# Token mixers that give way to the dense products half as often, in a two-layer hybrid encoder

## The chip, the core and the metric

The kernel runs on one core of one Trainium2 chip. The metric is the device time of one execution in microseconds (us), as the median of several runs. The kernel works on five engines: TensorE (PE in the profile; PEld is its weight load), VectorE (DVE), ScalarE (ACT), GpSimd (POOL) and SyncE (SP, which only issues DMAs here).

## The reference, cut to what matters

Input and output are 512 tokens of 1024 float32 numbers. Two layers follow one another, and a last RMSNorm. Each layer runs four token mixers A, B, C and D side by side on one projection, merges them by gates, and adds an MLP:

```python
for l in range(DEPTH):                       # DEPTH = 2
    xn = rmsnorm(x, norm1_g[l])
    h = xn @ w_in[l]                         # 1024 -> all mixers' inputs, split by columns
    y_a = gdn_mixer(...)                     # gated DeltaNet, both directions, 4 heads of 128
    y_b = diff_mixer(b_q, b_k, b_v, ...)     # softmax minus lam * softmax, 4 heads, full attention
    y_c = swa_mixer(c_q, c_k, c_v, ...)      # +-128 window, 8 query heads on 2 kv heads, sinks
    y_d = mlstm_mixer(...)                   # matrix memory, both directions, 4 heads
    branch = einsum('bsnw,nwd->bsnd', stack([y_a, y_b, y_c, y_d]), w_branch[l])
    gate = sigmoid(einsum('bsd,dne->bsne', xn, w_gate[l]))
    x = x + sum(gate * branch, axis=2) @ w_out[l]
    xn = rmsnorm(x, norm2_g[l])
    x = x + square(relu(xn @ w_mlp1[l])) @ w_mlp2[l]      # 1024 -> 4096 -> 1024
```

For the parts of the kernel that the change touches: the mLSTM (D) weighs `exp(decay) * (q k)` for each pair of tokens, multiplies it with v, and divides by a norm; B takes two softmax maps per head, p0 - lam p1, times v; C is a softmax over a band of up to three blocks of 128 keys, times v. B and D end with an RMSNorm over each head.

## The kernel before, in words

**Two streams on one TensorE.** The first stream is the dense one: the input projection, gates, branch projections, output projection and MLP, cut into *items*. Each product is taken in three passes over a high and a low part of both factors (lines 441, 442, 443 for moving tiles of 512 columns, lines 398, 399, 400 for 256 columns). Weights come from memory by DMA into one of two buffers `wr` (line 281), ACT rounds them to `wh` (line 298), DVE takes the rest `wl` (line 299). An item yields after each small group of its matmuls: mostly 6 of 512 columns or 12 of 256. The second stream is the mixers, generators that issue a few small matmuls (128 to 512 columns) with the ACT, DVE and POOL work around them, and then yield a number of nanoseconds.

**What sets the order.** `drive` (line 347) steps a mixer; the number that it yields goes to `fill` (line 332), which adds it to a debt and issues dense groups until the debt is paid. A larger number makes the next dense stretch longer. The numbers stand in the table `G` (`dh=1000`, `ds=1500`, `b1=900`, `b2=1100`, `b3=700`, `c=950`, `ce=1100`, `ss=300`). After that a scheduler orders the instructions on each engine by their order of issue and by when their operands are expected, so ACT, DVE and POOL rows can also move when only the yields change. Finished head norms of B go into a list `pend` and are transposed (`y_T`, line 1146, its matmuls line 1149) a few dense groups later. PSUM is shared by two pools of four banks: `pd` for the dense stream and `pm` for the mixers.

**The mixers, in the order in which they run in each layer (lines 1692 to 1702).** A (line 1157) has a loop `ss` that squares 8 tiles and adds them up by matmuls, and yields after each (line 1202). D (line 1446): for each head, four *s* groups (lines 1486, 1487: the score tile; 1493: the exps `W` on ACT; 1496: the product with the scores on DVE), each followed by a yield (line 1498), and four *hout* groups of the head before (line 1460: 10 small matmuls in all for one block of 128 tokens; 1462 to 1467: division by the norm, into `hs`), each followed by a yield (line 1468). After the last hout, the head norm (lines 1134 to 1145: squares on POOL 1138, sums on DVE 1140, a root on DVE 233 and POOL 234, products on DVE 1142 and 1143) and four `y_T`. B (line 1515) runs twice, for two heads each (B0 and B1 below), over 8 units: `front` (1529, 1530 scores; 1531 maximum on DVE; 1533 exps on ACT), three units later `mid` (1544 transposes, 1546 copy `at` on ACT), five units later `back` (1555 product with v, 1557 `bo` on ACT), with a yield after each. C (line 1583) does the same with 32 units: `front` (1591, 1592; exps 1599; POOL 1603 scales `cp`), three units later `mid` (1615) and `back`.

**Projections beside them.** Rotary inputs of B and C are evacuated by ACT (line 1013, four copies per bank), DVE (1014, 1015), POOL (1016) and put away by ACT and DVE (1024 to 1033).

Of the kernel before, what the change touches and what calls it, by code (L numbers as in the profile page):

```python
# [115 lines left out]
def encoder(ctx: ExitStack, tc: tile.TileContext, a: dict, out: bass.AP, dbg: dict = None):  # L116
# [1040 lines left out]
    def mixer_a(l, L):  # L1157
# [39 lines left out]
        for i, (src, w0) in enumerate(((kb, 72), (qb, 8))):  # L1197
            for h in range(4):
                sq = A(s="sq")
                act.activation(sq, src[:, h, :], AF.Square)  # L1200
                mm(ss, C["ssel"][:, w0 - h:w0 - h + P], sq, start=(i == 0 and h == 0), stop=(i == 1 and h == 3))
                yield G['ss']
        lnr = A(s="lnr")
        act.activation(lnr, ss, AF.Ln, scale=colc(2), bias=colc(7))
        gA = L.gA
# [240 lines left out]
    def mixer_d(l, L):  # L1446
        vx, EM, mb = L.vx, L.EM, L.mb
        qs, kh, kl = [[t[:, h, :] for h in range(4)] for t in (L.dq, L.dkh, L.dkl)]
        hsum = [A(s="hs") for _ in range(NT)]
        Ws = {}  # L1450

        def hout(h):
            W = Ws.pop(h)
            for t in range(NT):
                hb = PSM()
                hv = hb.rearrange("p (d c) -> p d c", d=2)
                for d in range(2):
                    js = range(0, t + 1) if d == 0 else range(t, NT)
                    for j in js:
                        mm(hv[:, d, 0:130], W[d][j][:, blk(t)], vx[:, j, h, :], start=(j == js[0]), stop=(j == js[-1]))  # L1460
                dn = SM(2, "dn")
                act.activation(dn, hv[:, :, 128], AF.Abs)
                dve.tensor_tensor(dn, dn, EM[:, t, h::4], op=ALU.max)
                dve.reciprocal(dn, dn)
                ho = hsum[t][:, blk(h)]
                act.activation(ho, hv[:, 0, 0:128], AF.Copy, scale=dn[:, 0:1])
                dve.scalar_tensor_tensor(ho, hv[:, 1, 0:128], dn[:, 1:2], ho, op0=ALU.mult, op1=ALU.add)
                yield G['dh']

        for h in range(4):  # L1470
            R, Rm = [], []
            for d in range(2):
                r = PSM()
                mm(r, oneh(0, d * 4 + h), L.RB1, start=True, stop=True)
                r1, r2 = A(s="R"), A(s="Rm")
                act.copy(r1, r)
                dve.tensor_tensor(m4(r2), m4(r), bmid(f(neg[1][:, d, :]), 4), op=ALU.add)
                R.append(r1)
                Rm.append(r2)
            yield G['dr']  # L1480
            W = [[None] * 4, [None] * 4]
            if h > 0:
                yield from hout(h - 1)
            for j in range(NT):
                s_ = PSM()
                mm(s_, kh[h][:, blk(j)], qs[h], start=True, stop=False)
                mm(s_, kl[h][:, blk(j)], qs[h], start=False, stop=True)
                for d in range(2):
                    ts_ = range(j, NT) if d == 0 else range(0, j + 1)
                    n = len(ts_)  # L1490
                    w_ = A(s="W") if n > 0 else None
                    for t in ts_:
                        act.activation(w_[:, blk(t)], (Rm if t == j else R)[d][:, blk(t)], AF.Exp,
                                       bias=mb[:, d, j, t, h:h + 1])
                    sl = slice(ts_[0] * P, (ts_[-1] + 1) * P)
                    dve.tensor_tensor(w_[:, sl], s_[:, sl], w_[:, sl], op=ALU.mult)
                    W[d][j] = w_
                yield G['ds']
            Ws[h] = W
        yield G['hl']  # L1500
        yield from hout(3)
        yT = ynew()
        L.y["d"] = yT
        ys = {}
        for tt in range(NT):
            ys[tt] = head_norm(hsum[tt], 4, L.og[:, tt, :].rearrange("p (h c) -> p h c", h=4))
            dump_y(f"yd{l}", ys[tt], 4, tt, 0)
            yield G['yn']
        yield G['yw']
        for tt in range(NT):  # L1510
            y_T(ys.pop(tt), 4, tt, 0, yT)
            yield G['yt']
        marks.add(f"yd{l}")

    def mixer_b(l, L, hp):
# [51 lines left out]
        for i in range(len(units) + b2):  # L1567
            if i < len(units):
                fr[i] = front(*units[i])
                yield G['b1']  # L1570
            if 0 <= i - b1 < len(units):
                md[i - b1] = mid(fr.pop(i - b1))
                yield G['b2']
            if 0 <= i - b2 < len(units):
                y = back(*units[i - b2], md.pop(i - b2))
                if y is not None:
                    pend.append([G['yp'], lambda y=y, u=units[i - b2]: y_T(y, 2, u[0], 2 * hp, yT)])
                yield G['b3']
        if hp == 1:
            L.y["b"] = yT  # L1580
            pend.append([0, lambda: marks.add(f"yb{l}")])
# [1 line left out]
    def mixer_c(l, L):  # L1583
# [60 lines left out]
        for i in range(len(units) + cl + 2):  # L1644
            if i < len(units):
                while f"cqT{units[i][0]}{l}" not in marks:
                    yield 1300
                fr[i] = front(*units[i])
                yield G['c']
            else:  # L1650
                yield G['ce']
            if 0 <= i - cl < len(units):
                mid(*units[i - cl], fr.pop(i - cl))
                yield G['c']
            j = i - cl - 1
            if 0 <= j < len(units) and units[j][2] == 3:
                u = units[j]
                back(u[0], u[1], u[3])
                yield G['c']
        L.y["c"] = yT  # L1660
        marks.add(f"yc{l}")

# [82 lines left out]
```

## Time and profile before

| | before |
|---|---|
| median of 3 runs | 2335.47 us (2334.99 to 2337.46) |
| profiled execution, its own time | 2333.33 us |
| its span, first to last instruction | 2331.6 us |
| granted TensorE clock, mean | 0.997 |
| PE busy | 2255.5 us (97%), 15944 instructions |
| PEld busy | 2014.0 us (86%) |
| DVE busy | 1605.4 us (69%) |
| ACT busy | 1237.9 us (53%) |
| POOL busy | 773.6 us (33%) |

A profile is of one execution. Its own time is what a sum over its rows is held against; between it and the median lie 2.1 us. In a timeline, a row is a run of like instructions on one engine: start, time from the first one's start to the last one's end, engine, line, what it writes and reads, how many, and in brackets how long the engine stood idle before it and which engine's result ended that. Matmuls overlap: a dense one of 512 columns lasts about 0.40 us in its row, and the next starts 0.23 us after it.

### The profile page before, as it was taken

The numbers are of one execution on the slowest core, as the hardware profiler recorded it, in microseconds if no ns is written. First come the engines' busy times: TensorE is split into PE (matmuls) and PEld (weight loads), VectorE is DVE, ScalarE is ACT, GpSimd is POOL, SyncE is SP. The second block draws the span as 40 slices with busy tenths as digits, with TensorE's granted clock in tenths as the row PEclk, the third lists the DMA queues.
The fourth block names the chain that finished last, engine by engine and source line by source line (L and its number), as shares of the span: only waits on it lengthen the run. The fifth ranks groups of instructions, "written<-read, shape, count | busy, mean of one in ns | idle before, by whom it ended". The sixth has DMA issues, their size and how long they took to land. (4 is left out here: it accounts for less than half of the span.)

```text
span 2331.6 us, 41278 instructions
## 1 busy us (share of the span) xinstructions
PE 2255.5 (97%) x15944; PEld 2014.0 (86%) x15944; DVE 1605.4 (69%) x2944; ACT 1237.9 (53%) x2827; POOL 773.6 (33%) x819
## 2 busy tenths in 40 slices
PE   7999999989999999999999999999999999999998
PEld 6879977878788989999987799878777889899998
DVE  5775547697885477677767745487877854877775
ACT  4565444766765264444445654367576633534443
POOL 1046552032332034443201655412313310444341
PEclk9999999999999999999999999999999999999999
DMA  6322131122122523233323112211322234233322
GB/s 154 94 53 64 56 95 60 55 92 81 56 66 83 162 73 120 90 104 115 107 80 91 55 56 64 91 55 55 100 73 64 64 113 136 88 99 109 100 83 91
DMA packets 234772, 200.81 MB, mean 86 GB/s; under 512 B 31824, under 2 KB 223696, under 8 KB 234576
## 3 DMA queue, kind: packets, MB, share of 16 engines
q1 hardware_dynamic: 231552, 193.09, 27.6%
q10 hardware_dynamic: 2304, 4.20, 0.5%
q8 instruction: 125, 2.05, 0.4%
q0 software_dynamic: 720, 0.89, 0.2%
q14 instruction: 71, 0.58, 0.1%
HBM read 190.25 MB, written 8.39 MB: 85 GB/s over the span
## 5 line engine op out<-in xcount | busy, mean ns | idle before, releaser
L299 DVE TENSOR_TENSOR wl<-wr,wh 128x512 fp32r<-128x512 f32 x540 | 412.1, 783 | 170.4 <-ACT wh L298 162.6
L298 ACT CAST wh<-wr 128x512 fp32r<-128x512 f32 x540 | 316.7, 620 | 222.9 <-PE pd L442 78.0
L441 PE MATMUL pd<-xh,wh 128*128 128x512 f32 (+1 forms) x768 | 307.9, 402 | 0.5 <-ACT xh L228 0.5
L442 PE MATMUL pd<-xl,wh 128*128 128x512 f32 (+1 forms) x768 | 297.3, 387 | 1.8 <-DVE xl L229 1.8
L443 PE MATMUL pd<-xh,wl 128*128 128x512 f32 (+1 forms) x768 | 298.6, 389 | 0.0
L399 PE MATMUL pd<-wl,hh 128*128 128x256 f32 x896 | 248.9, 278 | 0.0
L400 PE MATMUL pd<-wh,hl 128*128 128x256 f32 x896 | 248.8, 278 | 0.0
L398 PE MATMUL pd<-wh,hh 128*128 128x256 f32 x896 | 248.8, 278 | 0.0
L298 ACT CAST wh<-wq 128x512 fp32r<-128x512 f32 x196 | 115.2, 619 | 221.9 <-PE pd L400 95.4
L299 DVE TENSOR_TENSOR wl<-wq,wh 128x512 fp32r<-128x512 f32 x196 | 181.3, 959 | 13.6 <-ACT wh L298 13.5
L818 POOL TENSOR_TENSOR wq<-wq,wq 128x512 f32<-128x512 f32 x84 | 124.8, 1494 | 163.4 <-DVE wl L299 153.2
L443 PEld LDWEIGHTS pd<-xh,wl 128*128 128x128 f32 x768 | 145.6, 190 | 29.8
L442 PEld LDWEIGHTS pd<-xl,wh 128*128 128x128 f32 x768 | 146.2, 190 | 26.3 <-DVE xl L229 2.8
L399 PEld LDWEIGHTS pd<-wl,hh 128*128 128x128 f32 x896 | 168.7, 188 | 0.0
L400 PEld LDWEIGHTS pd<-wh,hl 128*128 128x128 f32 x896 | 168.7, 188 | 0.0
L398 PEld LDWEIGHTS pd<-wh,hh 128*128 128x128 f32 x896 | 168.2, 188 | 0.0
L441 PEld LDWEIGHTS pd<-xh,wh 128*128 128x128 f32 x768 | 145.8, 190 | 23.4 <-ACT xh L228 0.9
L686 DVE TENSOR_TENSOR x<-pd,x 128x512 f32<-128x512 f32 x124 | 85.1, 689 | 100.6 <-PE pd L400 100.5
L398 PE MATMUL pd<-wh,xh 128*128 128x256 f32 x512 | 149.6, 292 | 0.0
L399 PE MATMUL pd<-wl,xh 128*128 128x256 f32 x512 | 145.0, 283 | 0.0
L400 PE MATMUL pd<-wh,xl 128*128 128x256 f32 x512 | 143.5, 280 | 0.0
L1016 POOL TENSOR_TENSOR r<-r,r 128x512 f32<-128x512 f32 x26 | 36.1, 1390 | 301.3 <-PE pd L443 123.9
(394 smaller groups left out, 6632.6 us busy)
## 6 DMA issues: line engine op xcount, KB each, us to landing
wr<-in_w_in SPq DMA_DIRECT2D x92, 512.0 KB
wr<-in_w_mlp SPq DMA_DIRECT2D x72, 512.0 KB
wr<-in_w_gate SPq DMA_DIRECT2D x64, 512.0 KB
wq<-in_w_mlp SPq DMA_DIRECT2D x56, 512.0 KB
wr<-in_w_branch SPq DMA_DIRECT2D x32, 512.0 KB
wr<-in_w_out SPq DMA_DIRECT2D x16, 512.0 KB
x<-in_x SPq DMA_DIRECT2D x16, 256.0 KB
gsd<-gs ACTq DMA_DIRECT2D x16, 256.0 KB
```

Of the source, the lines that this page charges most:

```text
L298: act.copy(wh[:, k:k + n], raw[:, k:k + n])
L299: dve.tensor_tensor(wl[:, k:k + n], raw[:, k:k + n], f(wh[:, k:k + n]), op=ALU.subtract)
L398: mm(o, th, wh[:, k4, :], start=(kt == 0 and tt % 2 == 0), stop=False)
L399: mm(o, th, wl[:, k4, :], start=False, stop=False)
L400: mm(o, tl, wh[:, k4, :], start=False, stop=(kt == kts - 1 and tt % 2 == 1))
L441: mm(o, w1_, xh[kt][:, sl], start=(kt == 0 and hi_ == 0), stop=False)
L442: mm(o, w1_, xl[kt][:, sl], start=False, stop=False)
L443: mm(o, w2_, xh[kt][:, sl], start=False, stop=last)
L686: dve.tensor_tensor(d, bank.rearrange("p (t c) -> p t c", t=2), d, op=ALU.add)
L818: pool.tensor_tensor(d[:, k:k + 2], x[:, k:k + 2], y[:, k:k + 2], op=op)
L1016: pool.tensor_tensor(t, t, sh, op=ALU.add)
```

## The change

Neighbouring yields are merged into one, of the summed amount. In A's `ss` loop and in D's two loops every second yield goes and the other is doubled; in B the yields behind `mid` and `back` become one behind `back` (that behind `front` stays); in C the two or three yields of a turn become one at its end. Nothing is computed otherwise, no instruction is added or removed, and each mixer asks for the same sum of dense work.

```diff
@@ -1199,7 +1199,8 @@
                 sq = A(s="sq")
                 act.activation(sq, src[:, h, :], AF.Square)
                 mm(ss, C["ssel"][:, w0 - h:w0 - h + P], sq, start=(i == 0 and h == 0), stop=(i == 1 and h == 3))
-                yield G['ss']
+                if h % 2:
+                    yield 2 * G['ss']
         lnr = A(s="lnr")
         act.activation(lnr, ss, AF.Ln, scale=colc(2), bias=colc(7))
         gA = L.gA
@@ -1465,7 +1466,8 @@
                 ho = hsum[t][:, blk(h)]
                 act.activation(ho, hv[:, 0, 0:128], AF.Copy, scale=dn[:, 0:1])
                 dve.scalar_tensor_tensor(ho, hv[:, 1, 0:128], dn[:, 1:2], ho, op0=ALU.mult, op1=ALU.add)
-                yield G['dh']
+                if t % 2:
+                    yield 2 * G['dh']
 
         for h in range(4):
             R, Rm = [], []
@@ -1495,7 +1497,8 @@
                     sl = slice(ts_[0] * P, (ts_[-1] + 1) * P)
                     dve.tensor_tensor(w_[:, sl], s_[:, sl], w_[:, sl], op=ALU.mult)
                     W[d][j] = w_
-                yield G['ds']
+                if j % 2:
+                    yield 2 * G['ds']
             Ws[h] = W
         yield G['hl']
         yield from hout(3)
@@ -1568,14 +1571,16 @@
             if i < len(units):
                 fr[i] = front(*units[i])
                 yield G['b1']
+            gap = 0
             if 0 <= i - b1 < len(units):
                 md[i - b1] = mid(fr.pop(i - b1))
-                yield G['b2']
+                gap += G['b2']
             if 0 <= i - b2 < len(units):
                 y = back(*units[i - b2], md.pop(i - b2))
                 if y is not None:
                     pend.append([G['yp'], lambda y=y, u=units[i - b2]: y_T(y, 2, u[0], 2 * hp, yT)])
-                yield G['b3']
+                gap += G['b3']
+            yield gap
         if hp == 1:
             L.y["b"] = yT
             pend.append([0, lambda: marks.add(f"yb{l}")])
@@ -1646,17 +1651,18 @@
                 while f"cqT{units[i][0]}{l}" not in marks:
                     yield 1300
                 fr[i] = front(*units[i])
-                yield G['c']
+                gap = G['c']
             else:
-                yield G['ce']
+                gap = G['ce']
             if 0 <= i - cl < len(units):
                 mid(*units[i - cl], fr.pop(i - cl))
-                yield G['c']
+                gap += G['c']
             j = i - cl - 1
             if 0 <= j < len(units) and units[j][2] == 3:
                 u = units[j]
                 back(u[0], u[1], u[3])
-                yield G['c']
+                gap += G['c']
+            yield gap
         L.y["c"] = yT
         marks.add(f"yc{l}")
```

In the order of the instructions on PE, small matmuls of the mixers (which write `pm` banks) and dense ones (which write `pd` banks) take turns: 1061 changes from one kind to the other before, 925 after, so that 68 bursts are merged into a neighbour. A's order on PE does not change: its eight `ss` matmuls already stood side by side.

The first place is ACT at the end of mixer D in layer 1. `W` are the exps of the last score group of the last head, `wh` a rounded weight tile, `r2` the evacuation of a projection of B, `hs` and `dn` belong to hout. Before:

```order
L1493 ACTIVATE W_869_5187<-R_841_5037,mb_164_1026 128x128 x2
L1493 ACTIVATE W_869_5187<-Rm_842_5038,mb_164_1026 128x128
L298 CAST wh_885_5284<-wr_814_4891 128x512 x2
L1013 COPY r2_872_5200<-pd_849_5084 32x512 x4
L1493 ACTIVATE W_875_5212<-Rm_839_5032,mb_164_1026 128x128
L1493 ACTIVATE W_876_5215<-R_841_5037,mb_164_1026 128x128 x3
L1493 ACTIVATE W_876_5215<-Rm_842_5038,mb_164_1026 128x128
L298 CAST wh_906_5396<-wr_830_4983 128x512
L1030 CAST bkh_870_5198<-r1_873_5201 64x512
```

After:

```order
L1495 ACTIVATE W_869_5187<-R_841_5037,mb_164_1026 128x128 x2
L1495 ACTIVATE W_869_5187<-Rm_842_5038,mb_164_1026 128x128
L1495 ACTIVATE W_871_5195<-Rm_839_5032,mb_164_1026 128x128
L1495 ACTIVATE W_872_5198<-R_841_5037,mb_164_1026 128x128 x3
L1495 ACTIVATE W_872_5198<-Rm_842_5038,mb_164_1026 128x128
L298 CAST wh_885_5284<-wr_814_4891 128x512 x2
L1013 COPY r2_875_5212<-pd_849_5084 32x512 x4
L1463 ACTIVATE dn_878_5241<-pm_877_5235 128x2
L1467 ACTIVATE hs_732_4531<-pm_877_5235,dn_878_5241 128x128
```

The exps of the last score group, which stood behind two weight casts and four copies, now stand ahead of them.

The second place is DVE a little later, in D's head norm. `sq` of number 894 is what the first `y_T` transposes, `wl_907` is the low part of a weight tile in two halves. Before (the first half of `wl_907` stands 17 rows further up):

```order
L233 TENSOR_SCALAR hv_896_5346<-hss_895_5344 128x4
L299 TENSOR_TENSOR wl_907_5397<-wr_830_4983,wh_906_5396 128x512
L1467 SCALAR_TENSOR_TENSOR hs_733_4532<-pm_881_5262,dn_882_5268,hs_733_4532 128x128
L1032 TENSOR_TENSOR bkl_871_5199<-r1_880_5254,bkh_870_5198 64x512
L1464 RECIPROCAL dn_891_5334<-dn_891_5334 128x2
L1032 TENSOR_TENSOR bkl_871_5199<-r1_880_5254,bkh_870_5198 64x512
L1033 CAST bkl_871_5199<-bkl_871_5199 64x512 x2
L1467 SCALAR_TENSOR_TENSOR hs_734_4533<-pm_888_5304,dn_889_5310,hs_734_4533 128x128
L1467 SCALAR_TENSOR_TENSOR hs_735_4534<-pm_890_5328,dn_891_5334,hs_735_4534 128x128
L1142 TENSOR_TENSOR sq_894_5342<-hs_732_4531,hr_897_5347 128x512
L1140 TENSOR_REDUCE hss_899_5366<-sq_898_5364 128x4
L1143 TENSOR_TENSOR sq_894_5342<-sq_894_5342,og_482_3037 128x512
```

After:

```order
L1468 SCALAR_TENSOR_TENSOR hs_734_4533<-pm_888_5304,dn_889_5310,hs_734_4533 128x128
L1033 CAST bkl_874_5211<-bkl_874_5211 64x512
L1468 SCALAR_TENSOR_TENSOR hs_735_4534<-pm_890_5316,dn_891_5322,hs_735_4534 128x128
L1143 TENSOR_TENSOR sq_894_5342<-sq_894_5342,og_482_3037 128x512
L233 TENSOR_SCALAR hv_900_5368<-hss_899_5366 128x4
L1140 TENSOR_REDUCE hss_903_5388<-sq_902_5386 128x4
L1142 TENSOR_TENSOR sq_898_5364<-hs_733_4532,hr_901_5369 128x512
L233 TENSOR_SCALAR hv_904_5390<-hss_903_5388 128x4
L299 TENSOR_TENSOR wl_907_5397<-wr_833_4995,wh_906_5396 128x512
L1143 TENSOR_TENSOR sq_898_5364<-sq_898_5364,og_482_3037 128x512
L1142 TENSOR_TENSOR sq_902_5386<-hs_734_4533,hr_905_5391 128x512
L299 TENSOR_TENSOR wl_907_5397<-wr_833_4995,wh_906_5396 128x512
```

Both halves of `wl_907` now stand behind the product that the first `y_T` waits for (`sq_894`, line 1143 in the profile's numbering), among the products for the second and third.

The third place is ACT at the change from B1 to C in layer 1. `cq` are queries of C that are put away, `bo` B's output blocks, `yh` the high part of a `y_T`. Before:

```order
L1557 ACTIVATE bo_1177_6750<-pm_1176_6749,bst_1125_6524 128x128
L1024 ACTIVATE cq_1173_6739<-r1_1175_6741 64x512 x2
L298 CAST wh_1218_6930<-wr_1119_6493 128x512
L1013 COPY r2_1184_6790<-pd_1144_6607 32x512 x4
L228 CAST yh_924_5528<-pm_1188_6806 128x2x128
L1557 ACTIVATE bo_1187_6800<-pm_1186_6799,bst_1136_6579 128x128
L298 CAST wh_1218_6930<-wr_1119_6493 128x512
L1557 ACTIVATE bo_1187_6800<-pm_1186_6799,bst_1152_6643 128x128
```

After:

```order
L1560 ACTIVATE bo_1174_6734<-pm_1173_6733,bst_1125_6524 128x128
L298 CAST wh_1218_6930<-wr_1119_6493 128x512
L1013 COPY r2_1184_6790<-pd_1148_6622 32x512 x4
L228 CAST yh_924_5528<-pm_1188_6806 128x2x128
L1560 ACTIVATE bo_1187_6800<-pm_1186_6799,bst_1136_6579 128x128
L1024 ACTIVATE cq_1175_6746<-r1_1177_6748 64x512 x2
L298 CAST wh_1218_6930<-wr_1119_6493 128x512
L1560 ACTIVATE bo_1187_6800<-pm_1186_6799,bst_1152_6643 128x128
```

The two casts to `cq` and the copies that stood ahead of `bo_1187` have parted: the casts now follow it.

On PE, B1's `back` now follows its `mid` at once, where 6 dense matmuls stood between them; its `y_T` keep their place in the dense stream, so 24 dense matmuls lie between a `back` and its `y_T` where 18 did. In C, a `mid` now follows its turn's `front` at once, where a dense group of 6 lay between them.

## Rows read from the trace of the kernel before

**Rows 1.** The page, busy time and instructions by engine.
```profile
PE 2255.5 (97%) x15944; PEld 2014.0 (86%) x15944; DVE 1605.4 (69%) x2944; ACT 1237.9 (53%) x2827; POOL 773.6 (33%) x819
```
**Rows 2.** Waits of PE by releaser: total us, times, longest us.
```profile
PE pm L1149 <- DVE hv L233: 10.1, 4, 3.6
...
PE pm L1149 <- DVE sq L1143: 5.0, 6, 1.4
PE pm L1544 <- ACT p L1533: 4.0, 6, 1.4
PE pm L1615 <- POOL cp L1603: 3.6, 2, 1.8
PE pm L1555 <- ACT bo L1557: 3.4, 3, 1.6
...
PE pm L1460 <- DVE W L1496: 2.6, 2, 1.3
```
**Rows 3.** Busy time by window, layer 1's C, then two D ends; PEclk is granted clock.
```profile
core 0: us, PE busy (x) PEld busy (x) DVE busy (x) ACT busy (x) POOL busy (x), PEclk, DMA share, GB/s
...
627.00:727.00 100.00, 100.00 (x495) 83.04 (x496) 79.55 (x292) 68.34 (x230) 35.89 (x39) 1.00 0.23 71
473.00:482.00 9.00, 5.72 (x40) 5.06 (x39) 8.40 (x17) 4.27 (x8) 5.34 (x5) 1.00 0.02 5
1624.00:1632.00 8.00, 4.36 (x32) 3.88 (x31) 7.40 (x16) 3.42 (x7) 4.59 (x5) 1.00 0.00 0
```
**Rows 4.** Timeline of PE around one hout burst of mixer D.
```profile
start us, us, engine line op out<-in xcount [idle before <-releaser]
...
420.49 0.40 PE L443 MATMUL pd<-yh,wl 128*128 128x512 f32 x1
420.73 1.28 PE L1460 MATMUL pm<-vx,W 128*128 128x130 f32 x10
421.76 0.48 PE L441 MATMUL pd<-yh,wh 128*128 128x512 f32 x1
422.08 0.39 PE L442 MATMUL pd<-yl,wh 128*128 128x512 f32 x1
...
423.23 0.94 PE L1460 MATMUL pm<-vx,W 128*128 128x130 f32 x7
```
**Rows 5.** Timeline of ACT at the end of mixer D.
```profile
454.89 1.13 ACT L298 CAST wh<-wr 128x512 fp32r<-128x512 f32 x2
456.04 2.35 ACT L1013 COPY r<-pd 32x512 f32<-32x512 f32 x4
458.42 0.40 ACT L1493 ACTIVATE W<-Rm,mb 128x128 f32<-128x128 f32 x1
```
**Rows 6.** Timeline of PE from the end of D to the first mid of B0.
```profile
460.76 1.16 PE L1460 MATMUL pm<-vx,W 128*128 128x130 f32 x8 [1.29 <-DVE W L1496]
...
477.36 0.63 PE L1149 MATMUL pm<-c_ident,sq 128*128 128x128 f32 x4 [3.28 <-DVE hv L233]
...
480.64 0.60 PE L1149 MATMUL pm<-c_ident,sq 128*128 128x128 f32 x4
...
496.53 0.66 PE L1544 MATMUL pm<-c_ident,p 128*128 128x128 f32 x4 [1.36 <-ACT p L1533]
```
**Rows 7.** Timeline of DVE in the head norm of D.
```profile
474.28 1.49 DVE L1142 TENSOR_TENSOR sq<-hs,hr 128x512 f32<-128x512 f32 x1
...
478.41 0.69 DVE L1142 TENSOR_TENSOR sq<-hs,hr 128x512 f32<-128x512 f32 x1 [0.53 <-POOL hr L234]
...
484.01 0.68 DVE L299 TENSOR_TENSOR wl<-wr,wh 128x512 fp32r<-128x512 f32 x1
```
**Rows 8.** Timeline of POOL beside it.
```profile
474.18 2.49 POOL L1138 TENSOR_TENSOR sq<-hs 128x512 f32<-128x512 f32 x2 [1.91 <-DVE hs L1467]
```
**Rows 9.** Timeline of ACT at the start of B0.
```profile
488.43 1.14 ACT L298 CAST wh<-wr 128x512 fp32r<-128x512 f32 x2 [2.88 <-DMA wr<-in_w_branch]
489.48 0.68 ACT L1533 ACTIVATE p<-pm,bst 128x512 f32<-128x512 f32 x1
```
**Rows 10.** Timeline of PE, end of B1 and start of C.
```profile
604.82 0.41 PE L1149 MATMUL pm<-c_ident,sq 128*128 128x128 f32 x2 [0.88 <-DVE bst L1535]
...
619.61 1.16 PE L1555 MATMUL pm<-bv,at 128*128 128x128 f32 x8 [1.60 <-ACT bo L1557]
...
626.96 0.44 PE L1615 MATMUL pm<-c_ident,cp 128*128 128x128 f32 x2 [1.79 <-POOL cp L1603]
```
**Rows 11.** Timeline of ACT at the start of C.
```profile
614.59 1.28 ACT L1024 ACTIVATE cq<-r 64x512 fp32r<-64x512 f32 x2 [0.78 <-POOL r L1016]
...
619.18 0.37 ACT L1557 ACTIVATE bo<-pm,bst 128x128 f32<-128x128 f32 x1
```

## The prediction

> **What bounds the kernel now.** I read four views, in this order. First the page's busy times: PE is busy for 2255.5 us of a span of 2331.6, 97%, and no other engine passes 90% [rows 1]. So whatever the change brings can only come out of the 3% in which PE stands still, out of matmuls that become shorter, or out of clock. Second the busy time by window: C of layer 1 has a stretch of 100.00 us in which PE is busy for 100.00 [rows 3]. There the small groups are hidden already, and a longer burst has nothing to win. Third the waits of PE [rows 2]: six releasers that belong to D, B and C wholly or in part add up to 10.1 + 5.0 + 4.0 + 3.6 + 3.4 + 2.6 = 28.7 us over both layers, some of it at mixer A's own transposes, whose order stays. This is about 1.2% of the time, and a bound on what better cover can give: 2333 - 29 = 2304. Fourth the timelines at the places where these waits stand: the end of D, the start of B0, the end of B1 and the start of C [rows 6, 10]. They stand at the changes from one mixer to the next, not in the bodies of the loops. What decides is therefore not the number of bursts but what moves at four places per layer, in both layers alike.
>
> **Term 1, the 68 merged switches.** A switch costs what a dense matmul between two small bursts costs more than one in a row. Ten small matmuls start at 420.73 and last 1.28 us, seven last 0.94 us, so one takes (1.28 - 0.94) / 3 = 0.113 us. From the burst's start to the second dense matmul behind it pass 422.08 - 420.73 = 1.35 us; ten small ones and one dense one, at the 0.24 us between 420.49 and 420.73, would make 1.37 [rows 4]. So the switch costs nothing that shows. The first dense matmul does stand for 422.08 - 421.76 = 0.32 us, 0.08 more than 0.24, but the last small one is that much shorter. I take 0. Bounds: 68 x 0.08 = 5.4 us gained if the 0.08 were real, and the same lost if a longer burst cost it once more.
>
> **Term 2, the end of D.** Before, the last four exps start at 458.42, behind two casts and four copies from 454.89, 3.5 us of ACT [rows 5]; PE waits 1.29 us for the W that follows from them [rows 6]. Now the exps stand ahead. PE also comes there sooner, since 6 to 12 dense matmuls move behind the bursts, so I take 0.5 us of the wait to stay and 0.8 to go. The larger wait is that of the first y_T, 3.28 us [rows 6]. hout's last burst comes 6 dense matmuls (1.4 us at 0.24, or half of that for those of 256 columns) and those 0.8 us earlier, so the first y_T starts 1.5 us earlier (bounds 0 and 3.3).
>
> Against this stands what DVE was given to do. Both halves of wl_907 move behind the first y_T's product. After that product DVE has a sum, a product, and the first half: about 3 x 0.69, with two small ones (0.3) and the 0.53 in which it waits for POOL's root, 2.9 us [rows 7]. PE gets from a y_T at 477.36 to the next at 480.64, and the first use of that half is the fourth dense matmul before this end: 480.64 - 477.36 - 4 x 0.24 = 2.3 us [rows 6]. So PE waits 0.6 us, and about 0.2 more at the second half: 0.8 us lost (bounds 0 and 2.7, the latter with the products of rows 7 at 1.49 instead of 0.69 us). From 1.5 remain 0.7 us.
>
> This product at 1.49 us runs while POOL squares at 474.18, one at 478.41 takes 0.69 us without it [rows 7, 8]. The Trainium skill speaks against the change here: by "GPSIMD Engine Reference", section 1 "Specifications", GpSimd shares its SBUF interfaces with VectorE and contends with instructions that have two SBUF inputs. The trace agrees, 1.49 against 0.69; by that rule each DVE product or split that the new order brings beside a POOL operation loses 0.8 us, and two of them per layer would make the sum 3.2 us worse.
>
> **Term 3, the start of B0.** ACT casts two weight halves at 488.43, after 2.88 us of waiting for their DMA, and the first exps stand behind them at 489.48 [rows 9]. That DMA's buffer comes free when DVE ends a split at 484.01 + 0.68 = 484.69, and lands 3.7 us later [rows 7, 9]. Ahead of this split DVE now does two halves more, 1.3 us, from a start that is 1.4 us earlier: the DMA lands as before. What PE has won in D it waits for here. The maxima on DVE now stand behind one half of the next split, 0.6 us, of which I let 0.35 reach PE's wait at 496.53, and one dense matmul (0.23) less stands ahead of that wait. So D and the start of B0 end together 0.6 us later (bounds: 0.7 earlier, if nothing there binds; 4 later, if the splits and their DMAs come late with the products at 1.49).
>
> **Term 4, B1's y_T.** PE waits 0.88 us at 604.82 [rows 10]. The back whose output it transposes now comes 6 dense matmuls, 1.4 us, earlier. The wait goes: 0.9 us gained (bounds 0 and 0.9). In B0 a back is followed by 8 dense matmuls instead of 6 and four small ones, which is the same length: 0.
>
> **Term 5, the start of C.** PE waits 1.60 us at 619.61 for bo to be read by ACT [rows 10]. Ahead of bo's reading at 619.18 stand two casts of cq that started at 614.59 and take 1.28 us [rows 11]. They move behind it: 1.3 us of the wait go. The next wait, 1.79 us at 626.96 for POOL's cp [rows 10], has three dense matmuls more ahead of it, 0.7 us, but its chain is not shorter and PE reaches it 1.3 us sooner; I take 0.1 off. Together 1.4 us gained (bounds 0 and 2.2). In the rest of C PE is never idle [rows 3], and mid comes at most 6 dense matmuls (1.4 us) nearer to a front issued three turns earlier: 0.
>
> **The sum.** A layer gains -0.6 + 0.9 + 1.4 = 1.7 us, two layers 3.4 us. Against the profiled execution's own 2333.33 us this is 2329.9; the median lies 2.1 us above that execution, so 2332.0 us, 0.15% less than before. 0.2%, 4.7 us, is about what a measurement of this kernel can tell from no change.
>
> **Rivals.**
> - *The switch is not free.* If each merged burst saves the 0.08 us of rows 4, 5.4 us go as well: 2326.6. For it: the 0.32 us is a measured distance. Against it: ten small and one dense together are no longer than in a row.
> - *D's gain stays.* If the DMA at 488.43 lands earlier with the rest, D and B0 gain 0.7 instead of losing 0.6 per layer: 2332.0 - 2.6 = 2329.4. For it: the buffer's split starts earlier. Against it: the two halves put ahead of it.
> - *D's splits come late (slower).* Place: DVE behind the first y_T's product. wl_907's last half frees a weight buffer; its DMA, the cast behind it on ACT, the next split and the DMA of rows 9 follow each other. If the products run at 1.49 us, both DMAs land up to 3.3 us later, the exps of B0 with them, and a layer loses 4 us instead of 0.6: 2332.0 + 6.8 = 2338.8. It decides from the point where the cast of rows 9 starts more than 1 us after PE's gain at the first y_T would allow, that is later than 489.5 in layer 1's time of before. For it: rows 7 and 8 show 1.49. Against it: POOL's squares lie ahead of these rows.
> - *Nothing comes of it.* The waits only move, 2335.5: ACT and DVE are in order, and what is put behind one wait makes the next. For it: term 3 shows that once.
>
> The clock is no term: PE's granted clock stays at 1.00 through its longest waits, 3.28 us and layer 2's 3.6 [rows 2, 3], and no wait grows beyond these in my sum.
>
> **Chances and range.** The forecast 0.50, the switch 0.12, D's gain kept 0.17, D's splits late 0.12, nothing 0.09. With +-3 us about each: faster by over 0.2% (below 2330.8) 0.50 x 0.33 + 0.12 x 0.9 + 0.17 x 0.65 = 0.38; slower by over 0.2% (above 2340.1) 0.12 x 0.4 and what no case of mine holds, 0.14 in all; within 0.2% 0.48. All good ends together give 2335.5 - 2 x (0.7 + 0.9 + 2.2) - 5.4 = 2322.5, all bad ones 2335.5 + 8 + 5.4 = 2348.9; leaving 1 in 10 out on each side I take 2325 to 2341.
>
> **What the changed kernel's profile would show.** PE's wait for W near 461 is 0.5 us or gone; the first y_T in D starts about 1.5 us earlier, and a new wait of PE on wl from line 299 stands behind it (none: term 2 gains 0.8). The cast before B0's exps starts within 0.5 us of 488.4; later by over 1 us speaks for the late splits, earlier for the kept gain. PE's waits of 604.82 and 619.61 fall below 0.4 us each. The dense matmul behind a small burst still stands for 0.32 us. I am wrong if the sum of PE's waits changes by less than 1 us or more than 10, or if busy PE time shrinks by more than 2 us, which would be the switch.

## The result, and the profile after

The changed kernel took 2353.36 us (median; 2351.06 to 2354.38) where the kernel before took 2335.23 in the same comparison: a ratio of 1.0078 [1.0066, 1.0090]. It is 18 us slower, outside the predicted range of 2325 to 2341. The profiled execution took 2351.06 us, its span 2349.3. The page's busy times, to be held against [rows 1]:

```profile
PE 2269.2 (97%) x15944; PEld 2024.4 (86%) x15944; DVE 1600.6 (68%) x2944; ACT 1236.8 (53%) x2827; POOL 774.6 (33%) x819
```

The number of instructions is the same on every engine. PE is busy for 13.7 us more, and DVE, ACT and POOL are not slower. PE's waits by releaser, against [rows 2]:

```profile
PE pm L1149 <- DVE sq L1143: 18.9, 16, 3.1
...
PE pm L1547 <- ACT p L1536: 5.1, 5, 1.7
PE pm L1620 <- POOL cp L1608: 5.0, 2, 2.5
PE pm L1149 <- DVE hv L233: 3.2, 2, 1.6
PE pm L1532 <- ACT p L1536: 2.1, 6, 0.6
...
PE pm L1558 <- ACT bo L1560: 1.6, 4, 0.5
```

The wait of line 1460 for W is gone. The `y_T` (line 1149) wait 16 times for their product where it was 6, though part of this is the old wait for hv, 10.1 us and now 3.2, under another releaser. All waits of the view together went only from 68.1 to 72.0 us. The rest of the loss must stand where PE counts as busy, and the windows show some of it (columns as in [rows 3]):

```profile
475.00:480.00 5.00, 4.94 (x23) 4.65 (x24) 4.17 (x8) 1.17 (x2) 3.20 (x3) 0.66 0.00 0
...
1765.00:1770.00 5.00, 4.37 (x16) 3.59 (x15) 3.29 (x8) 3.32 (x9) 0.61 (x1) 0.53 0.42 117
```

Behind the first `y_T` of D the granted clock is 0.66 in the mean of 5 us, and in B1 of layer 2 it is 0.53. In shorter windows the level is 0.50 (1.2 GHz) or 1.00 (2.4 GHz): 0.50 for 10.2 us of the profile before, and for 34.1 us now (up to PE's last matmul).

Where the time went is told by stretches of PE's work that hold the same matmuls in both kernels (start of a named instruction to start of another, layer 1 / layer 2, us):

| stretch | before | after | change |
|---|---|---|---|
| D's start to its first y_T | 87.05 / 87.11 | 85.28 / 85.25 | -1.8 / -1.9 |
| first y_T to B0's first front | 8.79 / 8.76 | 12.72 / 13.90 | +3.9 / +5.1 |
| B0's first to last front | 27.50 / 27.38 | 26.59 / 25.92 | -0.9 / -1.5 |
| B0's last front to B1's first | 56.30 / 56.02 | 59.20 / 59.04 | +2.9 / +3.0 |
| B1's first front to C's first | 47.20 / 47.27 | 48.07 / 50.86 | +0.9 / +3.6 |
| C's first front to its last back | 108.79 / 108.62 | 110.94 / 109.13 | +2.2 / +0.5 |

These sum to 16.1 of the 17.7 us between the two spans. A good 10 us lie between B0's last front and C's first. Before, the two layers agree within 0.3 us in each stretch and none of these stretches has half clock. After, some have it, and not alike in both layers: 3.4 and 6.8 us between the first `y_T` and B0's first front, none and 6.8 in B1, 3.4 and none in C. The 59.2 and 59.0 us have none.

### The profile page after: what moved, and what is told of

It reads as the page before. It is cut to its first block, busy times and chain, and to the rows that moved or that the text cites. A ratio compares the mean times of both kernels' runs of the same rounds, so it can differ in the third digit from the quotient of the medians.

```text
span 2349.3 us, 41257 instructions
## 1 busy us (share of the span) xinstructions
PE 2269.2 (97%) x15944; PEld 2024.4 (86%) x15944; DVE 1600.6 (68%) x2944; ACT 1236.8 (53%) x2827; POOL 774.6 (33%) x819
## 5 line engine op out<-in xcount | busy, mean ns | idle before, releaser
L299 DVE TENSOR_TENSOR wl<-wr,wh 128x512 fp32r<-128x512 f32 x540 | 406.2, 772 | 184.9 <-ACT wh L298 179.5
```

Source lines behind the costliest of these rows:

```text
L299: dve.tensor_tensor(wl[:, k:k + n], raw[:, k:k + n], f(wh[:, k:k + n]), op=ALU.subtract)
```

## What the trace shows at these places

**B1.** PE in layer 1, where before the last `y_T` of this place waited 0.88 us [rows 10]:

```profile
608.02 0.66 PE L1547 MATMUL pm<-c_ident,p 128*128 128x128 f32 x4 [1.66 <-ACT p L1536]
...
609.11 0.30 PE L1149 MATMUL pm<-c_ident,sq 128*128 128x128 f32 x1 [0.43 <-ACT p L1536]
```

This mid is the sixth of eight and its own exps are long done. The exps named behind the arrow are those of the eighth front. What the mid lacks is a bank, since nothing else ties it to these exps: there are four `pm` banks, taken in turn, and its turn falls on the one that the eighth front's first scores hold until ACT's exp has read them. The `y_T`, which reads no `p` at all, waits in the same way for the bank of the second scores. ACT makes these exps late, and DVE shows why:

```profile
607.19 0.69 ACT L1536 ACTIVATE p<-pm,bst 128x512 f32<-128x512 f32 x1 [2.81 <-DVE bst L1534]
```
```profile
606.13 0.42 DVE L1142 TENSOR_TENSOR sq<-bo,hr 128x256 f32<-128x256 f32 x1 [0.60 <-POOL hr L234]
606.47 0.69 DVE L1534 TENSOR_REDUCE bst<-pm 128x1 f32<-128x512 f32 x1
```

The first row is ACT, the others DVE. The eighth front's scores were on PE from 600.85, but the maximum over them (line 1534) starts at 606.47: it is queued behind the head norm's product (line 1142), which waits for POOL's root. The same two instructions in the kernel before stood the other way round:

```profile
601.73 0.68 DVE L1531 TENSOR_REDUCE bst<-pm 128x1 f32<-128x512 f32 x1
...
603.31 0.43 DVE L1142 TENSOR_TENSOR sq<-bo,hr 128x256 f32<-128x256 f32 x1 [0.23 <-POOL hr L234]
```

Because the merged `back` is issued a yield earlier, its head norm is scheduled earlier too and goes into DVE's queue ahead of the next front's maxima.

**B0.** The `y_T` come nearer to their back. PE in layer 1 after the change:

```profile
518.72 0.41 PE L1149 MATMUL pm<-c_ident,sq 128*128 128x128 f32 x2 [0.56 <-DVE sq L1143]
...
526.97 0.41 PE L1149 MATMUL pm<-c_ident,sq 128*128 128x128 f32 x2 [0.86 <-DVE sq L1143]
...
535.33 0.41 PE L1149 MATMUL pm<-c_ident,sq 128*128 128x128 f32 x2 [0.67 <-DVE sq L1143]
...
540.11 0.41 PE L1149 MATMUL pm<-c_ident,sq 128*128 128x128 f32 x2 [0.23 <-DVE sq L1143]
```

Before, only the first of the four waited (0.58). Counted from the back whose output it reads, the first had 17 dense and 20 small matmuls ahead of it, now 13 and 16; the second 18 and 32, now 12 and 12; the third 24 and 18, now 12 and 16; the fourth 30, now 18. The order holds a `y_T` back by a count of groups of the dense stream (yp = 4), and a merged yield puts fewer bursts between.

**The end of D.** PE, against [rows 6]:

```profile
475.06 1.05 PE L1149 MATMUL pm<-c_ident,sq 128*128 128x128 f32 x4 [2.95 <-DVE sq L1143]
...
485.93 0.63 PE L1149 MATMUL pm<-c_ident,sq 128*128 128x128 f32 x4 [2.19 <-DVE sq L1143]
...
497.26 0.66 PE L1547 MATMUL pm<-c_ident,p 128*128 128x128 f32 x4 [0.70 <-ACT p L1536]
```

The first `y_T` comes 2.3 us sooner in time of the trace (1.8 by the stretch), but the fourth now waits 2.19 us. DVE, against [rows 7]:

```profile
477.64 0.69 DVE L299 TENSOR_TENSOR wl<-wr,wh 128x512 fp32r<-128x512 f32 x1
...
479.84 0.68 DVE L299 TENSOR_TENSOR wl<-wr,wh 128x512 fp32r<-128x512 f32 x1
...
481.04 0.68 DVE L1140 TENSOR_REDUCE hss<-sq 128x4 f32<-128x512 f32 x1
...
483.89 0.69 DVE L1142 TENSOR_TENSOR sq<-hs,hr 128x512 f32<-128x512 f32 x1 [0.90 <-POOL hr L234]
...
485.10 0.69 DVE L1143 TENSOR_TENSOR sq<-sq,og 128x512 f32<-128x512 f32 x1
```

Both halves of `wl_907` and the fourth head norm's sum (line 1140) are done between the other products, and the product the fourth `y_T` waits for ends at 485.79. It had itself waited 0.90 us for POOL's root.

**The start of C.** PE, against [rows 10]:

```profile
622.80 1.16 PE L1558 MATMUL pm<-bv,at 128*128 128x128 f32 x8 [0.53 <-ACT bo L1560]
...
631.80 0.44 PE L1620 MATMUL pm<-c_ident,cp 128*128 128x128 f32 x2 [2.50 <-POOL cp L1608]
```

The wait for bo fell from 1.60 to 0.53, and the one for cp rose from 1.79 to 2.50.

## The experiments

All ratios are to the kernel before on the same chip; its median is given for each comparison.

**One part at a time** (before: 2334.36). Each holds only one mixer's edits of the diff:

```diff
d_only:  hout, Ws   - yield G['dh']      + if t % 2: yield 2 * G['dh']   (and so for 'ds')
b_only:  mixer_b    - yield G['b2'] ... yield G['b3']    + gap += ...; yield gap
c_only:  mixer_c    - yield G['c'] ... yield G['c']      + gap += ...; yield gap
```

> Only the two edits in mixer D. Theory (waits and clock): the changed kernel loses at a few places after which PE runs at half clock; of its 17.7 us, the trace puts some 5.5 between D's start and B0's first front over both layers (a new wait of 2.2 us at the fourth y_T, half-clock stretches behind the first). So +4 to +8 us over the kernel before. Rival (each merged burst has a price): 26 of 68 bursts, 26 x 0.26 = +6.8 us, spread over D's body.

> Only the edit in mixer B. Theory (waits and clock): new waits at B0's y_T (1.8 us per layer) and at B1's last transposes (1.7 + 0.4 us in place of 1.1 per layer), and half clock behind some of them: +4 to +9 us over the kernel before. Rival (price per burst): 6 of 68 bursts, 6 x 0.26 = +1.6 us.

> Only the edit in mixer C. Theory (waits and clock): the wait at the first mid grows by 0.7 us per layer, with half clock behind it at times: +1 to +5 us over the kernel before. Rival (price per burst): 34 of 68 bursts, 34 x 0.26 = +8.8 us.

d_only: 2339.21, 1.0019 [1.0010, 1.0029]. b_only: 2346.75, 1.0049 [1.0034, 1.0064]. c_only: 2337.29, 1.0011 [1.0001, 1.0020]. The losses, 4.9 + 12.4 + 2.9 = 20.2 us, make up the 18 within their intervals. B is the largest part, more than I expected. c_only holds half of all merged bursts (34) and costs 2.9 us where 0.26 us for each would be 8.8: that price is out, though one of 0.08 would fit c_only alone. (A's edit alone was not run; up to D's start PE, DVE, ACT and POOL have the same order in both traces, and D starts 0.5 us earlier after.)

**Is it the clock?** Matmuls whose result is overwritten are put ahead of a waiting burst, in its own PSUM bank, so that PE does not stand still there. after_warm puts them into D, B1 and C of the changed kernel, after_warm_d into D alone, before_warm into D and the MLP (11 of them) of the kernel before:

```diff
+ def warm(ps, n):
+     for _ in range(n): mm(ps, identr, C["negr"][:, 0:512], start=True, stop=True)
  after_warm:   y_T of D + (12, 0, 0, 8)[tt]; mid of B1, unit 5 + 6; C's first mid + 10
  after_warm_d: y_T of D + (12, 0, 0, 8)[tt]
  before_warm:  y_T of D + (12, 0, 0, 0)[tt]; MLP, fg 1, e 2 + 11
```

> The changed kernel with matmuls that nothing reads (a constant of 512 columns, into the bank that the transposes behind them overwrite) in four waits of each layer: 12 before D's first y_T, 8 before its fourth, 6 before B1's sixth mid, 10 before C's first mid; at 0.232 us each they fit the waits of 2.95, 2.19, 1.66 and 2.5 us. Order of all else as in the changed kernel but for one y_T in B1. Theory (waits and clock): PE no longer stands still there, the half-clock stretches behind these waits go, 6 or 7 of 10 of 1.7 us each: -8 to -12 us against the changed kernel, 2341 to 2345. Rival (price per burst): the clock is not the cause, 2353 or more.

> The changed kernel with fillers (matmuls that nothing reads) in D's waits alone, 12 ahead of its first and 8 ahead of its fourth y_T, the rest of PE's order as in the changed kernel; the half-clock stretches behind these waits should go (9.4 of the 34 us of half clock in its profile). Theory (at D's end DVE's chain is the bound, and half clock hides behind it): as the changed kernel, 2352 to 2354. Rival (half clock costs in full there): 9.4 x 0.5 = -4.7, 2348.5.

> The kernel before with matmuls that nothing reads put into waits that it has itself: 12 ahead of D's first y_T (wait of 3.28 and 3.64 us) and 11 ahead of the third Strassen product of the MLP (2.89 and 2.76 us), in both layers. The clock fell to half behind both MLP waits in the profiled run, and in other runs behind the y_T. Theory (half clock costs its time where PE is the bound): two to four stretches less of 1.7 us, 2328 to 2331. Rival (half clock is hidden, PE would wait there in any case): 2334 +- 1; the fillers fit the waits.

after_warm: 2351.82, 1.0070 [1.0053, 1.0087], before 2334.36; 13.7 us at 0.50 instead of 34.1. after_warm_d: 2352.61, 1.0075 [1.0059, 1.0091], before 2334.88. before_warm: 2332.61, 0.9993 [0.9983, 1.0002], before 2334.45. My expectation of 8 to 12 us from the clock failed: 1.5 us came, less than the runs of either kernel spread (over 3 us). But this is no clean measure of the clock, since C's fillers cost time: at full clock C took 111.8 and 110.9, where the changed kernel's layer 2, at full clock too, took 109.1. after_warm_d at the end of D, window and PE:

```profile
474.00:480.00 6.00, 5.00 (x32) 3.87 (x31) 5.17 (x9) 1.50 (x3) 4.31 (x4) 1.00 0.00 0
```
```profile
475.17 0.63 PE L1154 MATMUL pm<-c_ident,sq 128*128 128x128 f32 x4 [0.19 <-DVE sq L1143]
...
478.49 0.50 PE L443 MATMUL pd<-xh,wl 128*128 128x512 f32 x1 [0.81 <-DVE wl L299]
...
486.03 0.63 PE L1154 MATMUL pm<-c_ident,sq 128*128 128x128 f32 x4 [0.49 <-DVE sq L1143]
```

The clock is at 1.00 throughout, and the `y_T` still start at 475.17 and 486.03, where they were at 475.06 and 485.93. From the first to the fourth `y_T` it is 10.86 us with the full clock and 10.87 with 3.4 us at half (layer 1). DVE sets the pace there; a slower PE only waits less. Behind the fourth `y_T` this is not so: layer 2 of the changed kernel has another 3.4 us at half there, and from first `y_T` to B0's front it took 13.90 us against 12.72 in after_warm_d. This is its fourth `y_T` and the window behind it:

```profile
1642.01 0.67 PE L1149 MATMUL pm<-c_ident,sq 128*128 128x128 f32 x4 [2.17 <-DVE sq L1143]
```
```profile
1642.00:1646.00 4.00, 3.99 (x13) 3.23 (x14) 3.32 (x6) 1.68 (x3) 0.00 (x0) 0.57 0.53 154
```

The half clock is paid for where no chain covers it. By the table, B1 took 50.86 us with 6.8 us of it and 48.07 without (48.40 in after_warm), and C 110.94 with 3.4 us of it and 109.13 without. With the 1.2 us behind the fourth `y_T` that is some 5.8 of this execution's 17.7 us: an estimate, since it takes the two layers as equal but for the clock. It stands behind waits that are new or grew, so order and clock are not separate causes here.

**What in B?** Three edits of b_only or the kernel before (before: 2334.45 for the first two, 2334.29 for the third):

```diff
b_yp6 (b_only):        - G: yp=4     + G: yp=6      (y_T two dense groups later)
b_late (b_only), before_late (before), in mixer_b:
- y = head_norm(o[:, :256], ...)     (inside back)
+ nq.append((o, unit))               (back only keeps o)
  ... front(*units[i]) ...
+ if nq: norm()                      (head_norm and its y_T, behind the next front)
```

> Mixer B merged as in b_only, and each y_T of B two dense groups further behind its back (yp 6 for 4). Theory: the merged yield brings back and y_T of B0 nearer in time, since fewer small bursts lie between them; with two groups more the three new waits of B0 (1.04 + 0.67 + 0.24 us per layer) go and B1's wait of 1.66 us stays: -3 to -6 us against b_only, 2341 to 2344. Rival (the merged bursts cost by themselves): as b_only, 2346.

> Mixer B merged as in b_only, but the head norm of a finished back is issued behind the next turn's front, so that DVE takes the front's maxima first, as in the kernel before. Theory: in b_only DVE stands in the head norm (waiting for POOL's root) while the maxima wait, the exps start 2.8 us late and PE waits 1.66 + 0.43 us for PSUM banks at B1's sixth mid; here that wait and the half clock behind it go, and B0's y_T come later too: -4 to -10 us against b_only, 2336 to 2342. Rival (merged bursts cost by themselves): 2346.

> The kernel before, nothing merged, with B's head norm issued behind the next turn's front. A control for b_late: theory (in the kernel before DVE already takes the maxima first, so the later head norm mends nothing there): 2333 to 2336. Rival (the later head norm is a gain of its own of some 6 to 10 us, which b_late only showed on top of the merge): 2324 to 2329.

b_yp6: 2340.57, 1.0025 [1.0014, 1.0036], 6.2 us below b_only. The near `y_T` of B0 are about half of the loss: the stretch to B1 is 56.6, in b_only 59.1. B1's `y_T` moved too, the last one into C. The mid of B1 still waits, on PE of b_yp6:

```profile
603.62 0.66 PE L1544 MATMUL pm<-c_ident,p 128*128 128x128 f32 x4 [1.68 <-ACT p L1533]
```

Its B1 takes 46.0 us in layer 2, which has no half clock there, with that wait in it (48.2 in b_only). So what the order of the maxima costs by itself is not separated by these runs; the table leaves it 0.9 us a layer, and the half clock behind it.

b_late: 2336.74, 1.0013 [1.0003, 1.0022], 10.0 us below b_only. It moves the `y_T` later along with the norm, so it undoes both effects: the stretch to B1 is 55.9 and 55.7. DVE of b_late in B1, then its PE:

```profile
601.35 1.28 DVE L1531 TENSOR_REDUCE bst<-pm 128x1 f32<-128x512 f32 x2
...
604.70 0.43 DVE L1142 TENSOR_TENSOR sq<-bo,hr 128x256 f32<-128x256 f32 x1 [0.62 <-POOL hr L234]
```
```profile
602.95 0.66 PE L1544 MATMUL pm<-c_ident,p 128*128 128x128 f32 x4
...
626.79 0.44 PE L1625 MATMUL pm<-c_ident,cp 128*128 128x128 f32 x2 [3.00 <-POOL cp L1613]
```

The maxima stand ahead of the product again and the mid waits for nothing; B1 takes 46.0 us, less than before's 47.2. But C's first mid waits 3.00 us and C takes 110.7 and 111.5, with 3.4 and 6.8 us at half clock behind that wait: what B1 saves C's start takes back. The control says the same: before_late, the late norm without any merge, is 2337.2, 1.0009 [1.0000, 1.0018], B1 at 45.7 and C at 111.0. So the late norm heals the merge and is no gain by itself.

**What in D?** (before: 2334.45 and 2334.29)

```diff
d_yt (d_only):        - yield G['yt']        + yield G['yt'] + (0, 0, 1300, -1300)[tt]
d_not_last (d_only):  - if t % 2:            + if h == 3 or t % 2:     (last head not merged)
```

> Mixer D merged as in d_only, and one dense group (6 matmuls, 1.4 us) moved from behind D's fourth y_T to ahead of it. Theory: D's end is bound by DVE's chain to the fourth y_T, with PE idle for 2.2 us there; the group fills 1.4 us of it: -2 to -3 us against d_only in both layers together, 2336 to 2337. Rival (the longer bursts of s and hout cost by themselves): 2339.

> Mixer D merged as in d_only but for the last head's s and hout groups, which keep a yield each; DVE's order at the end of D is then that of the kernel before, while 18 of d_only's 26 merged bursts stay. Theory (the loss is DVE's order at D's end, both weight halves and the fourth sum put behind the head norm's products): as the kernel before, 2334 to 2335.5. Rival (merged bursts cost by themselves): 18/26 of d_only's +4.7, 2337.6.

d_yt: 2338.94, 1.0022 [1.0012, 1.0032], no better than d_only. The fourth `y_T` waits 0.83 us instead of 2.1, and the next front takes it over:

```profile
485.60 0.63 PE L1149 MATMUL pm<-c_ident,sq 128*128 128x128 f32 x4 [0.83 <-DVE sq L1143]
...
491.12 0.47 PE L1531 MATMUL pm<-bkh,bq 128*128 128x512 f32 x1 [2.09 <-DVE yl L229]
```

More dense work ahead of PE's wait does not help when DVE's chain is the bound. d_not_last, with before's order at the last head, is 2336.63, 1.0006 [0.9996, 1.0015], and 18 of D's 26 merges are still in it. From D's start to B0's last front it takes 123.5 and 122.4 us, d_only 125.2, the kernel before 123.3. So the loss stands at the last head. It has before's order back on PE and DVE together; that DVE's is the part that counts is read from the rows above and not tested alone.

**All together, and C** (before: 2334.29 for after_fix and before_late_warm, 2334.88 for the others). after_fix is the changed kernel with d_not_last's and b_late's edits; fix_c adds 12 dense matmuls ahead of C's first mid, fix_c_warm adds before_warm's fillers too; before_c adds one dense group there to the kernel before; before_late_warm is before_late with before_warm's fillers:

```diff
fix_c (after_fix):  - yield gap         + yield gap + (2600 if i == cl - 1 else 0)
before_c (before):  - yield G['c']      + yield G['c'] + (1300 if i == cl - 1 else 0)
```

> The changed kernel with two places mended: D's last head keeps its yields, and B's head norm is issued behind the next turn's front. A, the rest of D, all of B's yields and C stay merged. Theory (two places where DVE's order changed carry the loss): 2353 - 4.7 - 10 = 2338, at most 2341. Rival (merged bursts cost by themselves): 2350 or more.

> after_fix with two dense groups (12 matmuls, 2.8 us) more ahead of C's first mid, where after_fix waits 2.99 us with half clock behind it; in after_fix C takes 2.7 us per layer more than before. Theory (the wait is a distance too short, and PE is the bound behind it, so that half clock costs there): -2 to -4 us per layer against after_fix, 2327 to 2331. Rival (the chain of C's start is the bound, the dense work is only missing later): 2334 to 2335.

> fix_c with the fillers of before_warm in D and the MLP. Theory: D's half clock is mostly hidden, the MLP's costs 1.7 us per layer: -1 to -4 us against fix_c, 2324 to 2329. Rival (half clock costs nothing anywhere): as fix_c.

> The kernel before, nothing merged, with one dense group (1.4 us) more ahead of C's first mid, where it waits 1.79 us. Theory: the wait goes by 1.4 us in each layer: 2331 to 2333. Rival (the chain of C's start is the bound): 2334 +- 1.

> before_late with the fillers of before_warm (12 matmuls ahead of D's first y_T, 11 ahead of the MLP's third product, read by nothing). Theory (half clock is mostly hidden behind DVE's chain at D's end, and costs its 1.7 us only behind the MLP's wait): as before_late less 1 to 3 us. Rival (half clock costs in full): less 5 to 6 us, since 6.4 us of lost clock went from before to before_warm.

after_fix: 2335.04, 0.9997 [0.9988, 1.0007]. The 18 us are gone with 54 of the 68 merges still there. PE's waits of after_fix:

```profile
PE pm L1628 <- POOL cp L1616: 6.0, 2, 3.0
...
PE pm L1149 <- DVE sq L1143: 4.1, 4, 1.4
...
PE pm L1547 <- ACT p L1536: 1.1, 2, 0.5
```

The mids and `y_T` no longer wait more than before; C's first mid does. fix_c: 2336.26, 1.0005 [0.9996, 1.0014]: the dense work takes 1.6 of that wait, and no time. fix_c_warm: 2332.80, 0.9992 [0.9983, 1.0001], 3.5 us below fix_c and the best of these, though not clearly better than the kernel before. before_late_warm: 2337.07, 1.0008 [0.9999, 1.0017], where the same fillers gain nothing. before_c: 2342.38, 1.0031 [1.0021, 1.0041], 7.5 us slower where I expected a gain. Its C takes 112.0 us instead of 108.8 at full clock, of which only 1.2 are the 5 more dense matmuls that now lie in C. (Its profiled execution is the fastest of its eight, 5 us below their median; the other seven ran at a lower mean clock.) The wait at the first mid is gone, and others came, on PE of before_c:

```profile
634.58 0.44 PE L1591 MATMUL pm<-ck,cq 128*128 128x384 f32 x1 [0.93 <-DVE ptl L229]
...
717.11 0.50 PE L1625 MATMUL pm<-pth,cv 128*128 128x512 f32 x1 [0.27 <-ACT pth L228]
```

B1's last `y_T`, held back by groups of dense work, now stands ahead of the front at 634.58, and before it stood behind it. The six product matmuls of a late back, from 716.13, take some 1.2 us longer. Why the splits (`pth`, `ptl`) are late there stays open, and with it why C's start is so sensitive.

## Why the prediction was wrong

- **Term 1, the switches: right within its bounds.** after_fix keeps 54 of the 68 merges and shows neither a price nor a gain; c_only keeps 34 and costs 2.9 us, of which its trace shows 1.8 in C and no cause for the rest. (The row of seven in [rows 4] is a burst of ten cut off at the edge of the window; the 0.113 us holds.)
- **Term 2, the end of D: half right.** The wait for W went, and the first `y_T` came 1.8 us earlier (1.5 predicted). The predicted new wait on `wl_907` shows as 0.81 us at its first half once PE is not slowed (after_warm_d; 0.6 predicted there, 0.8 with the second half). What I missed is the fourth `y_T`: I followed DVE to the first use of `wl_907` and not to the last product behind it, whose wait is 2.19 us.
- **Term 3, the start of B0: mis-sized.** D and B0's fronts together end 1.2 and 1.8 us later (0.6 predicted, up to 4 allowed), about 1.2 of the 1.8 by the half clock behind the fourth `y_T`. It is a late chain on DVE, as in the rival that I gave 0.12, but not by that rival's path: the cast ahead of B0's exps starts at 488.81, within the 0.5 us of 488.4 that I had set. The chain is made late by two splits and a sum in front of the fourth `y_T`'s product. After, this is the cast on ACT, then rows of DVE and POOL that lie beside each other:

```profile
488.81 1.14 ACT L298 CAST wh<-wr 128x512 fp32r<-128x512 f32 x2 [1.62 <-DVE yl L229]
```
```profile
473.77 1.15 DVE L1143 TENSOR_TENSOR sq<-sq,og 128x512 f32<-128x512 f32 x1
...
482.30 0.69 DVE L299 TENSOR_TENSOR wl<-wr,wh 128x512 fp32r<-128x512 f32 x1
```
```profile
473.09 2.72 POOL L1138 TENSOR_TENSOR sq<-hs 128x512 f32<-128x512 f32 x2 [2.49 <-DVE hs L1468]
...
482.47 1.38 POOL L234 TENSOR_TENSOR hr<-hv,c_col 128x4 f32<-128x4 f32 x1 [3.28 <-DVE hv L233]
```

  A product beside POOL's squares takes 1.15 us where others take 0.69, a split beside POOL's root takes 0.69. So the loss of 0.8 us that the Trainium skill ("GPSIMD Engine Reference", section 1 "Specifications") would have added for each product or split beside a POOL operation shows in part beside the squares and not beside the root; the products at 483.89 and 485.10 ran at 0.69 with nothing on POOL beside them.
- **Term 4, B: the step that failed.** I wrote 0.9 us gained in B1 and 0 in B0. B0 lost 2.9 and 3.0 us, B1 0.9 and 3.6, of which 2.8 are the half clock that only layer 2 has. For B1 I saw only that the back comes 6 dense matmuls earlier on PE. That its head norm moves on DVE too, ahead of the next front's maxima, I did not look up, though the order shows it: the `y_T`'s wait went from 0.88 to 0.43 us and the mid's from 0.17 to 1.66. Of the edits of the order only the one that issues the norm later (b_late, and the kernels that include it) took the mid's wait away, and 10 us came back, the distance undone with it. For B0 I counted the distance for one turn, and from the wrong back: the 8 and 6 dense matmuls stand behind the third, and the `y_T` there reads the second. The later `y_T` lost 6 to 12 dense matmuls, and b_yp6 gave 6 us back.
- **Term 5, the start of C: not a gain.** The wait for bo fell by 1.07 us as said (1.3 predicted), and the next one grew by 0.7; C lost 2.2 and 0.5, the 2.2 with 3.4 us of half clock. I took 0.1 off a wait whose chain I had called not shorter. fix_c shows that more dense work ahead takes 1.6 us of such a wait and gains no time.
- **"The clock is no term": wrong.** 24 us more at 0.50 came. Part of it lies under a chain of DVE and cost nothing (after_warm_d); the rest cost some 5.8 us of the profiled execution, by the estimate above. The reason that I gave was not in the rows: 3.28 and 3.6 us are not PE's longest waits (line 493 waits 8.6 us), and before, waits of 3.2, 2.9 and 2.8 us at 154.68, 863.63 and 2014.48 are each followed by 3.4 us at 0.50. One of them, PE and window of before:

```profile
863.63 0.38 PE L843 MATMUL pm<-xh,wl 128*128 128x256 f32 x1 [2.89 <-DVE wl L299]
```
```profile
865.00:868.40 3.40, 3.40 (x18) 3.40 (x17) 3.40 (x4) 1.01 (x2) 2.94 (x2) 0.50 0.00 0
```

- The test by waits would have misled: their sum changed by 4 us, within the 1 to 10 that I allowed, and the time by 18, since what was lost shows as stretched busy time and as gaps too short to be recorded waits.

## What to carry to other kernels

When bursts are merged, the work that hangs on a burst can move on every engine: print the in-order queue of the engine that feeds PE (here DVE) and look which short, urgent instruction (a maximum that an exp waits for) now stands behind a long chain with a wait in it. A distance that is counted in groups of other work shrinks when the groups in between are merged; count it for each turn, not for the first, and from the burst whose output is read. And compare equal stretches of work between two traces, since waits and busy time each show only a part of a loss.

## What was not expected of the hardware

Of the waits of PE between 2.2 and 3.6 us, some were followed by a granted clock of 0.50 and some not, in the same kernel and at the same place. After, the fourth `y_T` of D waits 2.19 us in layer 1 and 2.17 in layer 2: from 485 to 490 the clock is 1.00, from 1642 to 1646 it is 0.57. Where a DVE chain sets the time, half the clock cost nothing that shows (10.87 against 10.86 us). In B1 6.8 us of it cost 2.8, in C 3.4 us cost 1.8, by the difference of the two layers.
